# Four edits in a two-block transformer kernel: a norm's multiply on VectorE, one way to split attention weights, a reordered projection tail, and one early weight request

## The chip, the cores and the metric

The kernel runs on one core of one Trainium2 chip. The time is device microseconds of one launch, from the first to the last instruction and what lies around them; a smaller time is better.

## The reference, cut to what matters

Two model blocks run one after the other in float32. The first ends in a mixture of experts and a final norm; the second has two layers, `l = 0` and `l = 1`, each with a joint projection, attention of three kinds, an output projection and a feed-forward part.

```
# end of the first block: experts' rows are added, then the final norm
x = x + _hierarchical_moe(_rmsnorm(x, g_ffn), ...)
return _rmsnorm(x, g_final)             # x * rsqrt(mean(x*x) + eps) * g

# second block, per layer
p = h @ w_in                            # one projection for all three kinds
q_a, kv_a, dq, dk, dv, gq, gk, gv = split(p)
# mla: 4 heads; diff: 4 heads of 2 score sets; gqa: 8 query heads on 2 key heads
s = einsum('bhgqd,bhkd->bhgqk', q, k) * scale
p = softmax(s, axis=-1)
o = einsum('bhgqk,bhkd->bhgqd', p, v)
...
x = x + gate * rms(merge(o...) @ w_out)
x = x + gate * rms((silu(h @ w_gate) * (h @ w_up)) @ w_down)
```

The second block works on 768 rows in layer 0 (512 tokens and 256 context rows, six tiles of 128) and, for queries, on 512 rows (four tiles) in layer 1.

## The kernel before, in words

**Products.** A float32 product is done as three TensorE matmuls on operands split into a rounded high part and a low part (`mm3`: L99 high by high, L100, L101 the two mixed ones). A weight chunk of 128x2048 comes by a DMA on SP's queue into a buffer `raw` (L70); ScalarE copies it to `whi` (L81), VectorE subtracts to get `wlo` (L82). There are three buffers each of `raw`, `whi` and `wlo`. `ahead` asks for a chunk and splits it before its user is written; the user then finds it. Activations are split by `split`: ScalarE copies the high part (L91), VectorE subtracts (L92), both reading the same PSUM tile.

**Order.** Each engine runs its instructions in one fixed order, which a scheduler decides when the kernel is built, from the order of the code, the dependencies and the pools of buffers. So an edit in one place can move rows on several engines.

**End of the first block** (`combine`, `final`, `turned` in `moe`). For each of four token tiles, `combine(t)` adds the experts' rows (L1077) and, for two halves of 512 columns, adds a product from PSUM (L1037), sums the squares on ScalarE (L164), multiplies by the gain of the final norm on GpSimd (L1039), and sums the squares again. `final(t)` turns the sums into scales by a chain of 128x1 and 128x2 operations on VectorE (L1045 to L1051, with `rinv` L149 to L159); `turned(t)` transposes the normed tile on TensorE (`trp`, L131) into the second block's `hTx`. These run interleaved with products for the context rows.

**The projection** (`project`). Weight chunks 0 to 7 of `w_in` each give columns of `p` for six row tiles (`rows(g, tiles, ev)`; product tiles `prj`). Rows are brought into form on VectorE (`rope2`: L1431 to L1434, names `grow`, `drow`, `rp`) and written to a scratch array in DRAM, from which attention loads them (`p_d`). At the tail, a generator `gen` makes the first attention head (unit 0): it loads its rows, transposes q and k (`tp<-ident,raw`) and splits them (`mhi`, `mlo`). Chunk 3 gives the differential keys, chunk 4 the differential values (`vrow`, L1699). In this stage PSUM has six or seven tiles for products and transposes.

**Attention** (`attention`, `pipeline`). A layer has 20 units (4 mla, 8 diff, 8 gqa). For each unit, `scores` makes `sn` in PSUM, VectorE takes the maximum (L1903, L1911), ScalarE the exponentials `pn` (L1906); `turned` transposes `pn` in groups of 128x512 into a PSUM tile `tp` and splits it; `products` multiplies the two parts by the values (`pv`, L1955). There are three PSUM tiles of the kind `tp`, two `sn`, one `pv`. A unit has seven groups in layer 0 and six in layer 1. A table decides how a group is split:

```
if self.SPLITS[6 if t0 else k]:
    e = self.copies[0]
    self.copies.append(self.copies.pop(0))
    nc.scalar.activation(e, p, AF.Copy)
    nc.vector.tensor_copy(eh, e)
    nc.gpsimd.tensor_tensor(el, e, eh.bitcast(F), op=OP.subtract)
else:
    self.split(eh, el, p)
```

In the first way ScalarE copies PSUM to SBUF (L1938), VectorE casts (L1939) and GpSimd subtracts (L1940): four of seven groups in layer 0 and three of six in layer 1, 140 groups in all. The other 120 go by `split`.

**Hand-over to the next layer** (`ffn`, then `post` and the next `project`). The feed-forward part ends with a skewed loop over row tiles: down product, residual and norm (`post`), transposition into the next layer's `hT`. With layer 0, the first products of the next projection (chunks of `w_in2[1]`) follow the tiles as they come; their weights are requested on SP's queue behind the residual rows (`raw<-x_d`, `raw<-c_d`, L1383).

Of the kernel before, what the change touches and what calls it, by code (L numbers as in the profile page):

```python
# [8 lines left out]
F = mybir.dt.float32  # L9
R = mybir.dt.float32r  # L10
I32 = mybir.dt.int32
AF = mybir.ActivationFunctionType
OP = mybir.AluOpType
# [24 lines left out]
class Kern:  # L38
# [734 lines left out]
    def moe(self):  # L773
        nc, ph, sm = self.nc, self.ph, self.small
# [85 lines left out]
        el = L[:, :, 4:20].rearrange("p t (g e) -> p t g e", g=4)  # L860
# [112 lines left out]
        def places():  # L973
# [3 lines left out]
        bufs = (ph.tile([128, 1], I32, name="pix"), *places(), self.s8("praw", [2048], F),  # L977
                [self.mm("pmm0"), self.mm("pmm1")])
# [26 lines left out]
        y15, g2 = [], []  # L1005
# [19 lines left out]
        def combine(t):  # L1025
            for k in range(2):
                self.tc.keep_in_program_order(self.add_rows(xr[t], g2[t][:, k], main[k][1][:, t]))
            if t < 2:
                self.first_w[5 + t] = self.pair(raws[5 + t], k=8, pin=True)
            if t < 3:  # L1030
                self.context_products((7, 5, 6)[t], self.first_w)
            for c in range(2):
                cs = slice(c * 512, c * 512 + 512)
                x = xr[t][:, cs]
                p = self.mm("cmb")
                nc.tensor.matmul(p, spread[:self.CAP, t], y15[0][:self.CAP, cs], start=True, stop=True)
                nc.vector.tensor_tensor(x, x, p, op=OP.add)  # L1037
                self.sumsq(x, 512, fss[:, t, 0, c:c + 1])
                nc.gpsimd.tensor_tensor(x, x, y15[1][:, cs], op=OP.mult)  # L1039
                self.sumsq(x, 512, fss[:, t, 1, c:c + 1])  # L1040

        def final(t):
# [460 lines left out]
    def project(self, l, hT, new, nq, gq, qa, factors, stages=()):  # L1503


        nc = self.nc
        p_d = self.p_d
        tiles = range(6) if l == 1 else range(4)

        def rows(g, tiles, evac, w=None):  # L1510
            wh, wl = w or self.W(self.i["w_in2"][l, g], k=8, steps=4 if g > 4 else 1)
            for t in tiles:
                p = self.mm("prj")[:, :256]
                ts = slice(t * 128, t * 128 + 128)
                for kt in range(8):
                    hi, lo = (h[kt // 4][:, kt % 4, ts] if isinstance(h, list) else h[:, kt, ts] for h in hT)
                    self.mm3(p, hi, lo, wh[:, kt], wl[:, kt], kt == 0, kt == 7)
                evac(t, p)
            return wh, wl
# [93 lines left out]
        for t0 in (0, 4):  # L1613
            n = min(4, 6 - t0)
            c = slice(t0 * 128, (t0 + n) * 128)
            for k in range(3):
                if k < 2 and t0 >= nq:
                    continue
                p = self.mm("trp")
# [8 lines left out]
        for t in range(nq):  # L1628
            p = self.mm("qb")[:, :384]
# [11 lines left out]
        for t in range(6):  # L1641
            p = self.mm("kvb")
# [4 lines left out]
            pe = kv[:, t:t + 1, 128:]  # L1647
            if t < 4:
                pe = self.small.tile([128, 1, 32], F, name="kpe", bufs=2)
# [10 lines left out]
        raw = self.wp.tile([128, 2048], F, name="raw", tag="raw", bufs=self.NRAW)  # L1660
# [26 lines left out]
                out(t, col, o.rearrange("p h d -> p (h d)"))  # L1687

        differential(3, self.DK)
        while True:  # L1690
            try:
                next(gen)
            except StopIteration as e:
                self.unit0 = e.value
                break

        def ev_v(t, p):
            o = self.t5("vrow")[:, :256]
            nc.scalar.activation(o, p, AF.Copy)  # L1699
            out(t, self.DV, o)  # L1700
        rows(4, tiles, ev_v)


    def load_rows(self, pool, name, col, n, tiles=6, tag="rw"):
# [51 lines left out]
    def attention(self, l, yB, ap, nq):  # L1756

        nc = self.nc
# [7 lines left out]
        for _ in range(2):  # L1766
            hi, lo = (self.wp.tile([128, 4, 512], R, name="pe" + nm, tag="w" + nm, bufs=self.NW) for nm in ("hi", "lo"))
            self.pairs8 += [(hi[:, j], lo[:, j]) for j in range(4)]
        raw = self.wp.tile([128, 4, 512], F, name="pe", tag="raw", bufs=self.NRAW)
        self.copies = [raw[:, j] for j in range(4)]  # L1770

        self.fold = ap.tile([128, 64], F, name="fold")
        nc.vector.tensor_tensor(self.fold, self.ident[:, :64], self.ident[:, 64:], op=OP.add)
# [83 lines left out]
            nc.vector.tensor_tensor(y, y, r[:, t, :, None].to_broadcast([128, 4, 64]), op=OP.mult)  # L1857
            nc.vector.tensor_tensor(y, y, gd[:, None, :].to_broadcast([128, 4, 64]), op=OP.mult)

    SPLITS = (1, 0, 1, 0, 1, 0, 1)
    LAG = 5

    def pipeline(self, units, nq, ap):


        nc = self.nc
# [53 lines left out]
        def turned(u):  # L1922

            P, rec = probs.pop(u)
            o = ap.tile([128, 768], F, name="oT", bufs=2)
            for t0, n, k0 in groups:
                N = n * 128
                for k in range(k0, 6, 512 // N):
                    p = self.mm("tp")
                    for a in range(512 // N):  # L1930
                        for t in range(n):
                            self.tr(p[:, a * N + t * 128:a * N + t * 128 + 128], P[t0 + t][:, (k + a - k0) * 128:(k + a - k0) * 128 + 128])
                    eh, el = self.pairs8[0]
                    self.pairs8.append(self.pairs8.pop(0))
                    if self.SPLITS[6 if t0 else k]:
                        e = self.copies[0]
                        self.copies.append(self.copies.pop(0))
                        nc.scalar.activation(e, p, AF.Copy)  # L1938
                        nc.vector.tensor_copy(eh, e)  # L1939
                        nc.gpsimd.tensor_tensor(el, e, eh.bitcast(F), op=OP.subtract)  # L1940
                    else:
                        self.split(eh, el, p)
                    parts.append((u, t0, N, k, k0, eh, el, o, rec))
                    yield

# [109 lines left out]
    def ffn(self, l, hT, hp, nq):  # L2055
        nc = self.nc
# [23 lines left out]
        with self.pool("f_w") as fp:  # L2080
# [32 lines left out]
                    begun.append(g)  # L2113

            parts = [(hids[g], weight(g)) for g in (9, 10)]
            xs = self.residuals(l, "f", nq)
            gt = self.gates(l, "f", nq, hp)
            turns = []
# [135 lines left out]
```

## Time and profile before

| what | value |
|---|---|
| three runs, in order of size | 2999.06, 3010.52, 3013.27 us (median 3010.52) |
| the profiled execution | 3001.12 us, span 2999.3 us |
| TensorE busy | 2852.1 us, 95% of the span |
| VectorE, ScalarE, GpSimd busy | 1768.6, 1296.2, 413.1 us |
| mean granted clock of TensorE | 0.975 of full speed |

Times in the rows are microseconds from the start of the span. PE is TensorE's matmul, PEld its weight load, DVE VectorE, ACT ScalarE, POOL GpSimd, SP the engine whose queue issues most DMAs. A row of a timeline gives start, length, engine, line, operation, output and inputs, and in brackets how long the engine had been idle and what ended that. What ended the idle time is written as `<-DVE pelo L92`: the engine, tile and line of the instruction whose semaphore came last.

### The profile page before, as it was taken

Reading aid. Unit: us, or ns where it says so; the run is one execution under the profiler, and the core shown is the slowest. Engines: PE = TensorE matmul, PEld = TensorE weight load, DVE = VectorE, ACT = ScalarE, POOL = GpSimd, SP = SyncE. Lnnn points to the kernel's source line nnn. Section 1 sums busy time; section 2 is a strip of 40 time slices with the busy share of each in tenths; the row PEclk is TensorE's granted clock in tenths of the full one; section 3 lists DMA queues with packets and bytes.
Section 4 is the critical chain, followed back from the end, with each engine's and each line's share of the span. In section 5 each row is a group of like instructions: output and inputs, shape, how many; then the busy total and the mean of one; then the engine's idle time right before and its main releaser. Section 6 shows DMA issues by size and latency. Waiting matters only on the chain. (4 is left out here: it accounts for less than half of the span.)

```text
span 2999.3 us, 44707 instructions
## 1 busy us (share of the span) xinstructions
PE 2852.1 (95%) x17896; PEld 2463.1 (82%) x17896; DVE 1768.6 (59%) x3239; ACT 1296.2 (43%) x2275; POOL 413.1 (14%) x430
## 2 busy tenths in 40 slices
PE   8999999999799988999999999999988999899998
PEld 6997777769788878887789888888788777888887
DVE  6653344346588877789857343434565787644445
ACT  3222243234477765388745111212342787432222
POOL 2200010000110023156410000000010454000000
PEclk9999999999899999999999999999989999899999
DMA  5443464364799972421013121211233310322221
GB/s 201 141 145 138 150 207 161 142 225 168 262 388 385 351 275 87 146 78 27 4 71 141 71 71 56 71 57 71 77 127 101 106 24 3 141 99 105 92 98 71
DMA packets 130084, 399.78 MB, mean 133 GB/s; under 512 B 62199, under 2 KB 74887, under 8 KB 93128
## 3 DMA queue, kind: packets, MB, share of 16 engines
q1 hardware_dynamic: 116206, 350.04, 32.7%
q0 software_dynamic: 13520, 46.55, 4.6%
q8 instruction: 143, 2.34, 0.3%
q14 instruction: 71, 0.58, 0.1%
q10 hardware_dynamic: 144, 0.26, 0.0%
HBM read 356.64 MB, written 39.39 MB: 132 GB/s over the span
## 5 line engine op out<-in xcount | busy, mean ns | idle before, releaser
L82 DVE TENSOR_TENSOR wlo<-raw,whi 128x2048 fp32r<-128x2048 f32 (+2 forms) x203 | 421.2, 2077 | 292.9 <-ACT whi L81 292.4
L81 ACT ACTIVATE whi<-raw 128x2048 fp32r<-128x2048 f32 (+2 forms) x203 | 351.4, 1739 | 493.7 <-PE fd L101 128.6
L101 PE MATMUL fg<-hT,wlo 128*128 128x512 f32 (+1 forms) x1120 | 386.4, 345 | 0.0
L100 PE MATMUL fg<-hT,whi 128*128 128x512 f32 (+1 forms) x1120 | 386.2, 345 | 0.0
L99 PE MATMUL fg<-hT,whi 128*128 128x512 f32 (+1 forms) x1120 | 386.2, 345 | 0.0
L99 PEld LDWEIGHTS fg<-hT,whi 128*128 128x128 f32 x1120 | 211.1, 189 | 29.3
L100 PEld LDWEIGHTS fg<-hT,whi 128*128 128x128 f32 x1120 | 210.7, 188 | 29.3
L101 PEld LDWEIGHTS fg<-hT,wlo 128*128 128x128 f32 x1120 | 210.8, 188 | 29.0
L1940 POOL TENSOR_TENSOR pelo<-pe,pehi 128x512 fp32r<-128x512 f32 x140 | 181.4, 1298 | 192.0 <-DVE pehi L1939 187.5
L2106 DVE TENSOR_TENSOR sg<-sg,fg 128x512 f32<-128x512 f32 (+1 forms) x70 | 40.1, 573 | 282.1 <-PE fg L101 282.1
L101 PE MATMUL fd<-whi,hl 128*128 128x512 f32 x440 | 173.2, 394 | 0.0
L100 PE MATMUL fd<-wlo,hh 128*128 128x512 f32 x440 | 172.5, 392 | 0.0
L99 PE MATMUL fd<-whi,hh 128*128 128x512 f32 x440 | 171.2, 389 | 0.0
L1903 DVE TENSOR_REDUCE smx<-sn 128x1 f32<-128x768 f32 x160 | 151.8, 950 | 19.1 <-PE sn L1897 18.3
L2073 DVE TENSOR_TENSOR acc<-acc,fd 128x512 f32<-128x512 f32 x180 | 120.8, 686 | 65.1 <-PE fd L101 65.1
L131 PE MATMUL tp<-ident,pn 128*128 128x128 f32 x960 | 150.8, 276 | 4.1 <-DVE pelo L92 2.8
L1906 ACT ACTIVATE pn<-sn,smx 128x768 f32<-128x768 f32 x160 | 144.0, 905 | 19.7 <-DVE smx L1903 16.1
L99 PE MATMUL eg<-whi,xt 128*96 128x256 f32 x512 | 147.0, 287 | 0.0
L100 PE MATMUL eg<-wlo,xt 128*96 128x256 f32 x512 | 145.1, 283 | 1.5 <-DVE wlo L82 1.5
L101 PE MATMUL eg<-whi,xt 128*96 128x256 f32 x512 | 144.9, 283 | 0.0
L82 DVE TENSOR_TENSOR wlo<-rawx,whi 128x2048 fp32r<-128x2048 f32 x58 | 133.0, 2292 | 20.0 <-ACT whi L81 20.0
L1955 PE MATMUL pv<-pehi,vp 128*128 128x512 f32 (+1 forms) x280 | 124.3, 447 | 8.7 <-ACT oT L1959 7.8
(658 smaller groups left out, 7552.0 us busy)
## 6 DMA issues: line engine op xcount, KB each, us to landing
raw<-in_w_in SPq DMA_DIRECT2D x53, 1024.0 KB, 5.3
raw<-in_w_ada SPq DMA_DIRECT2D x48, 1024.0 KB, 5.1
raw<-in_f_gate SPq DMA_DIRECT2D x22, 1024.0 KB, 4.8
raw<-in_f_up SPq DMA_DIRECT2D x22, 1024.0 KB, 4.8
raw<-in_f_down SPq DMA_DIRECT2D x22, 1024.0 KB, 4.8
rawx<-in_e_gate SPq DMA_DIRECT2D x19, 1024.0 KB, 9.1
rawx<-in_e_up SPq DMA_DIRECT2D x19, 1024.0 KB, 9.0
rawx<-in_e_down SPq DMA_DIRECT2D x18, 1024.0 KB, 8.6
```

Source lines behind the costliest of these rows:

```text
L81: keep(nc.scalar.activation(hi[:, c], raw[:, c], AF.Copy))
L82: keep((eng or nc.vector).tensor_tensor(lo[:, c], raw[:, c], hi[:, c].bitcast(F), op=OP.subtract))
L99: t.matmul(ps, lh, rh, start=first, stop=False)
L100: t.matmul(ps, lh, rl, start=False, stop=False)
L101: t.matmul(ps, ll, rh, start=False, stop=last)
L131: self.nc.tensor.transpose(out, in_, self.ident[:k, :k])
L1903: nc.vector.tensor_reduce(m[:, t:t + 1], p[:, :768], axis=AX.X, op=OP.max, negate=True)
L1906: nc.scalar.activation(P[t], p[:, :768], AF.Exp, bias=m[:, t:t + 1], accum_out=su[:, t:t + 1])
L1940: nc.gpsimd.tensor_tensor(el, e, eh.bitcast(F), op=OP.subtract)
L1955: nc.tensor.matmul(p, v[:, k + a], e[:, a * N:a * N + N], start=k == k0 and a == 0 and e is eh, stop=k + a == 5 and e is el)
L2073: nc.vector.tensor_tensor(acc[:, t, cs], acc[:, t, cs], p, op=OP.add)
L2106: nc.vector.tensor_tensor(sg, sg, pp[1], op=OP.mult)
```

## The change

1. In `combine` the multiply by the final norm's gain goes from GpSimd to VectorE.
2. In `pipeline` the table and the three-engine way are gone: all groups go by `split`. The `raw` buffer that held the copies is not taken.
3. In `project` the values (chunk 4) are written ahead of the rest of the first head's generator, which advances one step after each of the last three row tiles, and runs to its end after them.
4. In `ffn` of layer 0, chunk 7 of the next `w_in` is asked for by `ahead` before the residual rows.

```
-                nc.gpsimd.tensor_tensor(x, x, y15[1][:, cs], op=OP.mult)
+                nc.vector.tensor_tensor(x, x, y15[1][:, cs], op=OP.mult)
...
         differential(3, self.DK)
-        while True:
-            try:
-                next(gen)
-            except StopIteration as e:
-                self.unit0 = e.value
-                break
...
-        rows(4, tiles, ev_v)
+
+        def first_head():
+            self.unit0 = yield from gen
+
+        head = first_head()
+        w = None
+        for t in tiles:
+            w = rows(4, [t], ev_v, w)
+            if t >= tiles[-1] - 2:
+                next(head, None)
+        for _ in head:
+            pass
...
-        raw = self.wp.tile([128, 4, 512], F, name="pe", tag="raw", bufs=self.NRAW)
-        self.copies = [raw[:, j] for j in range(4)]
...
-    SPLITS = (1, 0, 1, 0, 1, 0, 1)
...
-                    if self.SPLITS[6 if t0 else k]:
-                        e = self.copies[0]
-                        self.copies.append(self.copies.pop(0))
-                        nc.scalar.activation(e, p, AF.Copy)
-                        nc.vector.tensor_copy(eh, e)
-                        nc.gpsimd.tensor_tensor(el, e, eh.bitcast(F), op=OP.subtract)
-                    else:
-                        self.split(eh, el, p)
+                    self.split(eh, el, p)
...
             parts = [(hids[g], weight(g)) for g in (9, 10)]
+            if l == 0:
+                self.ahead(("w_in2", (1, 7), 8))
             xs = self.residuals(l, "f", nq)
```

What the edits do to the order of rows, at three places. First VectorE, inside one diff unit of layer 0's attention; `pelo` is a group's low part, `pehi` its high part, `pe` the copy in SBUF, `smx` a row maximum. Before:

```order
1307 L1919 RECIPROCAL srec<-ssum 128x6
1308 L1903 TENSOR_REDUCE smx<-sn 128x1
1309 L1939 CAST pehi<-pe 128x512 x2
1310 L92 TENSOR_TENSOR pelo<-tp,pehi 128x512
1311 L1903 TENSOR_REDUCE smx<-sn 128x1
1312 L1939 CAST pehi<-pe 128x512
1313 L1903 TENSOR_REDUCE smx<-sn 128x1
```

And after, at the same place of the next diff unit:

```order
1309 L1919 RECIPROCAL srec<-ssum 128x6
1310 L92 TENSOR_TENSOR pelo<-tp,pehi 128x512 x2
1311 L1903 TENSOR_REDUCE smx<-sn 128x1
1312 L92 TENSOR_TENSOR pelo<-tp,pehi 128x512
1313 L1903 TENSOR_REDUCE smx<-sn 128x1
1314 L92 TENSOR_TENSOR pelo<-tp,pehi 128x512
1315 L1903 TENSOR_REDUCE smx<-sn 128x1
```

Every cast has become a subtraction that reads the PSUM tile; the maxima stand between them as before.

Second TensorE, at layer 0's projection tail; `tp<-ident,raw` transposes the first head's rows, `prj` are the products. Before, all twelve stood together ahead of the 96 value products that close the projection:

```order
6856 L100 MATMUL prj<-wlo,hTx 128x256
6857 L101 MATMUL prj<-whi,hTx 128x256
6858 L131 MATMUL tp<-ident,raw 96x128 x12
6859 L99 MATMUL prj<-whi,hTx 128x256
6860 L100 MATMUL prj<-wlo,hTx 128x256
```

After, the first four come behind 48 products of the values (which stood from row 6859 on before), two behind the next 24, and the last six behind another 24. The first of the three places:

```order
6905 L100 MATMUL prj<-wlo,hTx 128x256
6906 L101 MATMUL prj<-whi,hTx 128x256
6907 L131 MATMUL tp<-ident,raw 96x128 x4
6908 L99 MATMUL prj<-whi,hTx 128x256
6909 L100 MATMUL prj<-wlo,hTx 128x256
```

The products of two row tiles have moved ahead of the first transposes.

Third SP's queue, at the end of layer 0's feed-forward part; `raw<-in_w_in` are the next projection's weights, `x_d` and `c_d` the residual rows. Before:

```order
360 L70 DMA raw<-in_f_down 128x2048 x2
361 L1383 DMA raw<-x_d 128x1024 x4
362 L1383 DMA raw<-c_d 128x1024 x2
363 L70 DMA raw<-in_w_in 128x2048 x6
364 L1522 DMA p_d<-gvrow 128x128 x5
```

And after:

```order
363 L70 DMA raw<-in_f_down 128x2048 x2
364 L70 DMA raw<-in_w_in 128x2048
365 L1383 DMA raw<-x_d 128x1024 x4
366 L1383 DMA raw<-c_d 128x1024 x2
367 L70 DMA raw<-in_w_in 128x2048 x6
```

One request has moved ahead of the residual rows, and six still stand behind them: chunk 7 is asked for twice, since its last two row tiles are written in a later call.

## Rows read from the trace of the kernel before

**Rows 1.** The page's first part: busy time, share, instructions by engine.

```profile
PE 2852.1 (95%) x17896; PEld 2463.1 (82%) x17896; DVE 1768.6 (59%) x3239; ACT 1296.2 (43%) x2275; POOL 413.1 (14%) x430
```

**Rows 2.** Waits of PE, whole span: total us, times, longest.

```profile
PE trp L131 <- ACT yg L1053: 6.8, 1, 6.8
...
PE prj L99 <- ACT whi L81: 5.2, 1, 5.2
...
PE pv L1955 <- POOL pelo L1940: 1.4, 1, 1.4
```

**Rows 3.** Busy time in the two attention stretches, layer 0 then layer 1.

```profile
1261.00:1531.00 270.00, 246.84 (x1684) 212.53 (x1684) 225.14 (x369) 218.37 (x497) 139.11 (x119) 0.99 0.17 45
2334.00:2553.00 219.00, 206.48 (x1326) 168.84 (x1326) 181.68 (x317) 175.21 (x357) 107.17 (x97) 0.99 0.17 48
```

**Rows 4.** The page's costliest groups: GpSimd's subtraction in attention.

```profile
L1940 POOL TENSOR_TENSOR pelo<-pe,pehi 128x512 fp32r<-128x512 f32 x140 | 181.4, 1298 | 192.0 <-DVE pehi L1939 187.5
```

**Rows 5.** VectorE's cast by line: shortest, median, longest in ns.

```profile
L1939 DVE CAST pehi<-pe x140: 382/421/1549, 1274.4 to 2547.4; 128x512 fp32r<-128x512 f32 x140
```

**Rows 6.** VectorE's groups in layer 0's attention: busy us, mean ns.

```profile
L1939 DVE CAST pehi<-pe 128x512 fp32r<-128x512 f32 x80 | 47.6, 600 | 7.0 <-ACT pe L1938 6.4
L92 DVE TENSOR_TENSOR pelo<-tp,pehi 128x512 fp32r<-128x512 f32 x60 | 40.8, 680 | 2.2 <-ACT pehi L91 2.1
```

**Rows 7.** The same in layer 1's attention.

```profile
L1939 DVE CAST pehi<-pe 128x512 fp32r<-128x512 f32 x60 | 28.1, 468 | 5.8 <-ACT pe L1938 5.2
L1800 DVE CAST dqst<-dqrow 128x256 fp32r<-128x256 f32 x8 | 8.5, 1066 | 0.0
...
L1800 DVE CAST dkst<-dkrow 128x384 fp32r<-128x384 f32 x8 | 2.8, 353 | 0.0
```

**Rows 8.** Waits of PE in layer 0's attention.

```profile
PE sn L1897 <- ACT pn L1906: 4.9, 10, 1.4
PE pv L1955 <- ACT oT L1959: 4.1, 3, 2.9
PE tp L129 <- DVE pelo L92: 3.3, 3, 1.4
PE tp L131 <- DVE pelo L92: 2.8, 4, 1.0
...
PE tp L1968 <- DVE pelo L92: 0.8, 2, 0.6
```

**Rows 9.** GpSimd's multiply at the first block's end, by line.

```profile
L1039 POOL TENSOR_TENSOR x<-x,y x8: 1260/1298/2314, 1111.7 to 1150.1; 128x512 f32<-128x512 f32 x8
```

**Rows 10.** VectorE's timeline there, and a 128x512 multiply later in the kernel.

```profile
1132.72 1.12 DVE L149 TENSOR_SCALAR fin_v<-fv 128x2 f32<-128x2 f32 x1
1133.88 0.17 DVE L150 TENSOR_SCALAR fin_y<-fin_v 128x2 int32<-128x2 int32 x1
...
2147.76 0.69 DVE L2078 TENSOR_TENSOR acc<-acc,gt 128x512 f32<-128x512 f32 x1
```

**Rows 11.** The projection tail, layer 0: busy time of one stretch, then PE.

```profile
1244.00:1248.00 4.00, 1.47 (x7) 0.88 (x8) 3.96 (x11) 0.75 (x2) 0.75 (x1) 0.88 0.50 172
...
1245.27 0.61 PE L131 MATMUL tp<-ident,raw 128*96 128x128 f32 x4 [2.04 <-DMA raw<-p_d]
```

**Rows 12.** The projection tail, layer 1: timelines of PE and DVE.

```profile
2310.57 1.06 PE L131 MATMUL tp<-ident,raw 128*96 128x128 f32 x4 [5.60 <-issue]
...
2309.65 0.42 DVE L1431 TENSOR_TENSOR drow<-prj,rope 128x256 f32<-128x256 f32 x1
```

**Rows 13.** The hand-over to layer 1: SP's queue, then ACT.

```profile
2164.02 42.66 SPq L70 DMA_DIRECT2D raw<-in_w_in  x6
...
2171.76 2.19 ACT L81 ACTIVATE whi<-raw 128x512 fp32r<-128x512 f32 x4 [3.19 <-DMA raw<-in_w_in]
2174.12 0.46 ACT L1369 ACTIVATE pre<-trp,mod,pre_a 128x128 f32<-128x128 f32 x1 [0.18 <-PE trp L131]
...
2200.49 2.18 ACT L81 ACTIVATE whi<-raw 128x512 fp32r<-128x512 f32 x4
```

## The prediction

> **What bounds the kernel now.** The page's first part comes first: TensorE is busy 95% of the span, VectorE 59% [rows 1]. Some 147 us of the 2999.3 us span are left in which TensorE does nothing, so edits that touch other engines can only pay where TensorE waits for them, or where its clock falls after a wait. The waits of TensorE tell where that is [rows 2]: one wait of 6.8 us for `yg` at the end of the first block, one of 5.2 us for the split of a weight chunk in the hand-over to layer 1, and a single one of 1.4 us for GpSimd's subtraction in attention, although that subtraction takes 181.4 us of GpSimd's time [rows 4]. GpSimd's own time there hides nearly whole. What remains is its effect on VectorE.
>
> Next the busy time in the two attention stretches [rows 3]. In 270.0 us of layer 0 TensorE is busy 246.8, VectorE 225.1, ScalarE 218.4; in 219.0 us of layer 1 it is 206.5, 181.7 and 175.2. So no engine is free: TensorE leads, the two others run at some 80%, and a unit's work passes from one to the other through three transposed tiles in PSUM. TensorE's idle time is 23.2 us in the one and 12.5 us in the other, 35.7 us together: no gain in attention can be much beyond that.
>
> **The norm's multiply.** Eight GpSimd operations of about 1.30 us (one 2.31) go [rows 9], and eight VectorE multiplies of one size with the 0.69 us of a later line come [rows 10]. VectorE gets 8 x 0.69 = 5.5 us more. Against this stand the places where VectorE was held: a 128x2 operation takes 0.17 us, and the same kind takes 1.12 us when it begins just after GpSimd's multiply [rows 10]. With some five such places of about 0.95 us that gives 4.8 us back; VectorE's sum is about even. The chain is what gets shorter: sum of squares, multiply, sum of squares runs twice per tile, and each multiply is 1.30 - 0.69 = 0.6 us shorter. Ahead of the 6.8 us wait for `yg` lie two multiplies of its own tile and two held operations: 2 x 0.6 + 2 x 0.95 = 3.1 us. The bounds are 0, if a multiply that queues on VectorE behind other work gives it all back, and 5 us if the half clock behind the wait shortens too. I take -3.
>
> **One way to split.** ScalarE does the same (a copy becomes a copy). GpSimd loses 140 subtractions. VectorE loses 140 casts and gets 140 subtractions of 0.68 us. The casts cost 600 ns in layer 0 and 468 ns in layer 1, means over 80 and 60 [rows 6, 7], while the shortest is 382 and the median 421 ns [rows 5]. So VectorE gets 80 x 0.08 + 60 x 0.21 = 6.4 + 12.8 = 19 us more. What it gets back: other casts that GpSimd holds, such as `dqst` at 1066 ns against 353 ns for the larger `dkst` in the same stretch, 8 x 0.71 = 5.7 us [rows 7]. The net is about +13 us of 407 us, on an engine with 82 us of idle time there [rows 3]: it fits.
>
> Two effects on TensorE are left. A PSUM tile was given back after ScalarE's copy, and now after VectorE's subtraction. In layer 0, the 60 groups that already go this way made TensorE wait 3.3 + 2.8 + 0.8 = 6.9 us [rows 8], 0.115 us a group; in layer 1 its waits hold none for that. For the 80 groups of layer 0 that change, this gives 80 x 0.115 = +9.2 us, for the 60 of layer 1 none. If the three tiles are now all held behind VectorE it may be twice that, +18. On the other side, VectorE is no longer held for up to 1.55 us by a neighbour (the longest cast), and its results come in steadier steps. The waits that hang on VectorE through ScalarE, `pn` and `oT`, are 4.9 + 4.1 us in layer 0 [rows 8], and the low part comes without GpSimd's 1.30 us [rows 4]; if these 9.0 us and the 1.4 us for GpSimd go, that is -10, and with the small stalls that no row names perhaps half of all idle time, -15. I take 0 between +18 and -15: the likely loss (+9) and the likely gain (-10) are of one size.
>
> The row of the longest cast shows a lock rather than a slower engine: 0.42 us alone, 1.3 to 1.55 us beside GpSimd [rows 5]. The Trainium skill, SBUF — State Buffer, section "Who interferes with whom", says that a VectorE cast in a two-port mode, or an operation with two SBUF inputs, is fully blocked while a GpSimd operation that reads SBUF holds the shared port, and that one with at most one SBUF input outside those modes is not. The trace agrees in the cast's two lengths; by that rule the subtraction from PSUM, with one SBUF input, is never held, and the first rival below would be the likelier outcome.
>
> **The values ahead of the first head.** In layer 0, TensorE is busy 1.47 of the 4 us from 1244 on, its first transposes having waited 2.04 us for a DMA, but VectorE is busy 3.96 of these 4 us [rows 11]. The products written ahead need a PSUM tile and a free row buffer each, and both come free through VectorE (`drow`). TensorE then does the products of two row tiles in place of the wait, and waits for VectorE behind them. In layer 1 the 5.60 us wait ends at 2310.57, just after VectorE's first `drow` operation of 0.42 us began at 2309.65 [rows 12]: what ended it was a PSUM tile. The value products need the same tile. So no gain there. The keys' splits now stand directly ahead of the first scores, which costs about one subtraction of 0.68 us [rows 6] in each layer. Bounds: -7.6 us (both waits, 2.0 + 5.6, hidden), +1.4 us (2 x 0.68); I take 0, the rows of VectorE being nearest.
>
> **The early weight request.** Before, the next layer's first chunk is requested at 2164.02 and split from 2171.76 on, in four steps that take ScalarE 2.19 us [rows 13], and TensorE waits 5.2 us for it [rows 2]. After, it lies ready, and products of the first two tiles fill this wait. But chunk 7 is still asked for a second time for its last two row tiles, and that split stands on ScalarE at the same place, ahead of the `pre` of 2174.12 [rows 13], which waits behind it in any case. The next transposes hang on that. What surely goes is the last of the splits ahead of the remaining products, the 2.18 us of 2200.49 [rows 13], which moves up by one request. I take -2; bounds 0 and -7.4 (5.2 + 2.2).
>
> **The sum.** -3 + 0 + 0 - 2 = -5 us. On the profiled execution of 3001.1 us this gives 2996. That execution and the three runs (2999.1, 3010.5, 3013.3) have a mean of 3006.0; less 5, 3001 us is my forecast. The three runs lie 14 us apart, 0.5%, so under 0.5% (15 us) a difference cannot be told from none; a "faster" must fall below 2995.5.
>
> **The rivals.** (A) Attention runs steadier: the lock on VectorE gone outweighs the longer hold of PSUM, -15 us in place of 0, 2986 us. For it: the 600 ns casts and their 1.55 us extreme [rows 5, 6]. Against: TensorE hardly waits on that path now [rows 2]. (B) The waits really are hidden, in the projections -7.6 and at the hand-over -7.4 in place of -2: -18 in all, 2988 us. Against: VectorE is full in one and PSUM holds the other [rows 11, 12]. (C) Slower: each transposed PSUM tile waits for VectorE's queue in attention, +18 us, and with -5 from the other parts the sum is +13, 3019 us; a median of 0.5% more, 3025.6, needs +25 in attention, 0.63 us in each of 40 units. For it: TensorE already waits 6.9 us on that path in layer 0 [rows 8]. It decides from the point at which a group costs over 0.115 us on 140 groups, 16 us. (D) Nothing comes through at all, 3006 us.
>
> **How the numbers follow.** The forecast, together with (D), has 0.48; (A) 0.24; (B) 0.13; (C) 0.15. (A) and (B) lie below 2995.5; a fifth of them may end above it, since runs spread by 0.5%, and a little of the forecast ends below it: 0.8 x 0.37 + 0.05 = 0.35 for faster. A half of (C) passes 3025.6, and the forecast's own spread adds a little: slower 0.10. The rest is within 0.5%: 0.55. The range reaches to (A) and (B) and 6 us below them, for both in part, and to (C); beyond it lie a fifth of the cases, those in which (A) and (B) come whole together or attention loses more than its bound: 2980 to 3020.
>
> **What the changed profile would show.** Right: the wait for `yg` near 4 us in place of 6.8; small VectorE operations there at 0.17 us throughout; no rows of GpSimd's subtraction, and `dqst` near 0.35 us; waits of TensorE for `pelo` in layer 0 grown from 6.9 to about 16 us, with those for `pn` and `oT` smaller, and the stretches' lengths near 270 and 219 us. The 2.0 and 5.6 us waits would be found again a few microseconds later, behind the value products. The 5.2 us wait goes, and a wait for `hT` takes its place. It would be wrong, above all, if the attention stretches change by over 10 us together, either way; or if TensorE's wait at either projection's tail is gone with none behind it.

## The result, and the profile after

The changed kernel takes 2976.5 us in the median of 12 runs (2969.5 to 2984.3), the kernel before 2998.6 us in the median of 12 (2990.1 to 3013.3). The ratio is 0.9913 with a 95% interval of 0.9895 to 0.9931: 0.9% faster, some 26 us on a kernel of 3000 us. The forecast was 3001 us, the range 2980 to 3020: too slow by 24 us, with the measured time 3.5 us below the range. Of these, 7 are in the base: the four executions from which it was taken have a mean of 3006.0, and 12 runs have a median of 2998.6. The rest is a change of -26 to -22 in place of -5. All ratios are of executions in the fast state; one execution, of 7079 us, is left out by that, with all but the split path.

The first part of the page of the changed kernel answers to [rows 1]:

```profile
PE 2847.3 (96%) x17896; PEld 2463.2 (83%) x17896; DVE 1766.0 (59%) x3244; ACT 1293.1 (43%) x2272; POOL 214.7 (7%) x282
```

GpSimd has lost 198 us. VectorE's busy time has not grown, although eight multiplies were moved to it and 140 casts became longer subtractions; the prediction had it grow by 13 us in attention alone.

Where the time went is read by stages: each from the start of its first product on TensorE to the start (or end) of a later one, in the timeline. Layer 0's attention, for example, lies between the first row of `sn` and the end of the last row of `pv`. In the kernel before:

```profile
1261.16 0.50 PE L1897 MATMUL sn<-mhi 96*128 96x512 f32 x1 [0.47 <-ACT vrow L1699]
...
1527.12 0.28 PE L1955 MATMUL pv<-pelo,vp 128*128 128x256 f32 x1
```

And in the changed kernel:

```profile
1254.96 0.50 PE L1897 MATMUL sn<-mhi 96*128 96x512 f32 x1 [1.52 <-DVE mlo L92]
...
1509.74 0.28 PE L1948 MATMUL pv<-pelo,vp 128*128 128x256 f32 x1
```

That is 266.2 us before (1527.12 + 0.28 - 1261.16) and 255.1 after. All stages that differ, taken so from the profiles, with a second profile of either kernel (runs described below) beside it:

| stage | before, twice | after, twice |
|---|---|---|
| norm: first `cmb` to first `prj` | 32.3, 32.3 | 28.4, 28.4 |
| projection of layer 0: first `prj` to first `sn` | 119.8, 121.5 | 119.9, 119.9 |
| attention of layer 0 | 266.2, 267.4 | 255.1, 255.3 |
| feed-forward of layer 0: first to last `fg` | 519.3, 518.7 | 525.7, 519.3 |
| hand-over: last `fg` to first `prj` of layer 1 | 40.4, 40.5 | 34.9, 35.0 |
| projection of layer 1: first `prj` to first `sn` | 161.7, 158.2 | 159.7, 159.3 |
| attention of layer 1 | 217.7, 217.7 | 212.5, 212.4 |

So the norm gives 3.9 us, layer 0's attention 11 to 12, layer 1's 5.3, and hand-over and projection of layer 1 together 4 to 7. The feed-forward stage of layer 0, of which no instruction was changed, took 519 or 526 us, within one kernel too; it is left out of the reasoning and comes back at the end.

In layer 0's attention these are the waits of TensorE in the changed kernel, to be laid beside [rows 8]:

```profile
PE sn L1897 <- ACT pn L1906: 5.9, 13, 1.5
PE sn L1897 <- DVE mlo L92: 1.5, 1, 1.5
PE pv L1948 <- ACT oT L1952: 1.3, 2, 0.9
PE tp L131 <- DMA mkrow<-p_d: 1.3, 1, 1.3
PE tp L131 <- DVE pelo L92: 0.9, 3, 0.5
```

The reader should see the last line. The wait for `pelo` was to grow from 6.9 us to about 16, since 140 groups give back their PSUM tile by that subtraction in place of 60. It has shrunk to 0.9. What VectorE does there, beside [rows 6]:

```profile
L92 DVE TENSOR_TENSOR pelo<-tp,pehi 128x512 fp32r<-128x512 f32 x140 | 94.3, 683 | 7.6 <-ACT pehi L91 7.0
...
L1803 DVE CAST dqst<-dqrow 128x384 fp32r<-128x384 f32 x8 | 3.2, 398 | 0.0
...
L1803 DVE CAST dkst<-dkrow 128x384 fp32r<-128x384 f32 x8 | 2.8, 350 | 0.0
```

In layer 1 the cast `dqst` went from 1066 ns [rows 7] to 487:

```profile
L1803 DVE CAST dqst<-dqrow 128x256 fp32r<-128x256 f32 x8 | 3.9, 487 | 0.0
```

The 140 subtractions all take 0.68 us, and the other casts have come down.

### The profile page after: what moved, and what is told of

The parts are those of the page before. It is cut to its first block, busy times and chain, and to the rows that moved or that the text cites. A ratio compares the mean times of both kernels' runs of the same rounds, so it can differ in the third digit from the quotient of the medians.

```text
span 2976.6 us, 44654 instructions
## 1 busy us (share of the span) xinstructions
PE 2847.3 (96%) x17896; PEld 2463.2 (83%) x17896; DVE 1766.0 (59%) x3244; ACT 1293.1 (43%) x2272; POOL 214.7 (7%) x282
## 5 line engine op out<-in xcount | busy, mean ns | idle before, releaser
L82 DVE TENSOR_TENSOR wlo<-raw,whi 128x2048 fp32r<-128x2048 f32 (+1 forms) x200 | 420.5, 2104 | 292.1 <-ACT whi L81 291.7
L81 ACT ACTIVATE whi<-raw 128x2048 fp32r<-128x2048 f32 (+1 forms) x200 | 351.0, 1762 | 495.0 <-PE fd L101 132.2
L92 DVE TENSOR_TENSOR pelo<-tp,pehi 128x512 fp32r<-128x512 f32 x260 | 175.0, 683 | 13.9 <-ACT pehi L91 11.8
L91 ACT ACTIVATE pehi<-tp 128x512 fp32r<-128x512 f32 x260 | 153.8, 601 | 44.9 <-PE tp L131 43.6
L1903 DVE TENSOR_REDUCE smx<-sn 128x1 f32<-128x768 f32 x160 | 151.7, 949 | 12.7 <-PE sn L1897 11.7
```

Source lines behind the costliest of these rows:

```text
L81: keep(nc.scalar.activation(hi[:, c], raw[:, c], AF.Copy))
L82: keep((eng or nc.vector).tensor_tensor(lo[:, c], raw[:, c], hi[:, c].bitcast(F), op=OP.subtract))
L91: nc.scalar.activation(hi, src, AF.Copy)
L92: nc.vector.tensor_tensor(lo, src, hi.bitcast(F), op=OP.subtract)
L1903: nc.vector.tensor_reduce(m[:, t:t + 1], p[:, :768], axis=AX.X, op=OP.max, negate=True)
```

## The experiments

The theory after the result (the **lock theory**): VectorE's operations whose inputs lie in SBUF were held while GpSimd worked, and the engine runs in order, so a held cast made the maxima and the subtractions behind it late; that was the cause of TensorE's waits for `pelo`. Two rivals: the **chain theory** (the low part comes sooner by two engines than by three) and the **buffer or order theory** (a free weight buffer, or another order of the rows on all engines). All ratios are to the kernel before, run on the same chip.

### One split path alone

```
-                    if self.SPLITS[6 if t0 else k]:
...
-                    else:
-                        self.split(eh, el, p)
+                    self.split(eh, el, p)
```

> The kernel before with the one split path alone (the raw buffer of the copies not taken either). If attention carries the change, as the stretches of the two traces say (11.2 us shorter in layer 0, 5.2 us in layer 1), this comes out 14 to 19 us below before. If the gain comes from the four parts together, through another order of the rows, it is under 8 us.

Measured: ratio 0.9942 (0.9922 to 0.9962), 17 us. Layer 0's attention took 254.8 us, as in the changed kernel; layer 1's 215.5, 2.2 less than before. So this part makes the gain in layer 0, and two thirds of the whole.

### All but the split path

```
+    SPLITS = (1, 0, 1, 0, 1, 0, 1)
...
+                    if self.SPLITS[6 if t0 else k]:
+                        e = self.copies[0]
```

> The changed kernel with the table and the three-engine way put back: norm, values first and early request remain. Attention theory: 3 to 7 us below before, the 3.9 us of the norm's stage and little else. Order theory: over 10 us below.

Measured: 0.9956 (0.994 to 0.9972), 13 us (8 to 18). This is more than the 3 to 7 us of the attention theory, and the number alone is that of the order theory (over 10). The stages say otherwise: the norm's stage is 28.4 us, layer 0's attention 263.5, hand-over and projection of layer 1 194.8 together (202.0 and 198.7 before), layer 1's attention 216.3. These are parts of some 4, 3 to 4, 4 to 7 and 1.4 us at the places of the three edits that remain and right behind them, which the prediction had at 5 together.

### The norm alone

```
-                nc.gpsimd.tensor_tensor(x, x, y15[1][:, cs], op=OP.mult)
+                nc.vector.tensor_tensor(x, x, y15[1][:, cs], op=OP.mult)
```

> The kernel before with the norm's multiply on VectorE alone. By the sum of the prediction 3 us below before; by the trace of the changed kernel 3.9 us in that stage. If this part carries less than 1 us, the stage's gain came from the other rows that moved there.

Measured: 0.9978 (0.9964 to 0.9993); its interval, 2 to 11 us, holds the 3.9 us by which the stage is shorter (28.4 us, in each of the eight profiles with this edit; 32.3 in each of the six without it). This is the changed kernel's VectorE at the place of [rows 10]:

```profile
1130.17 0.16 DVE L157 TENSOR_TENSOR fin_t<-fin_y 128x2 f32<-128x2 f32 x1
1130.25 0.68 DVE L1039 TENSOR_TENSOR x<-x,y 128x512 f32<-128x512 f32 x1
1130.85 0.15 DVE L158 TENSOR_TENSOR fin_t<-fin_t,fin_v 128x2 f32<-128x2 f32 x1
```

And TensorE's wait, 6.8 us before [rows 2]:

```profile
1132.92 1.94 PE L131 MATMUL trp<-ident,yg 128*128 128x128 f32 x8 [5.30 <-DVE yg L1062]
1135.04 0.58 PE L99 MATMUL prj<-whi,hTx 128*128 128x256 f32 x1 [0.19 <-ACT hTx L1374]
```

The multiply takes 0.68 us and the small operations beside it 0.16: none is held.

### The cast from PSUM, with GpSimd kept

This takes the lock from the 140 casts and leaves the three engines in their chain: VectorE makes the high part as the maximum of the PSUM tile and its copy, which is the same value, and has one input in SBUF.

```
-                        nc.vector.tensor_copy(eh, e)
+                        nc.vector.tensor_tensor(eh, p, e, op=OP.max)
                         nc.gpsimd.tensor_tensor(el, e, eh.bitcast(F), op=OP.subtract)
```

> The kernel before, with the three engines kept (ScalarE copies, VectorE makes the high part, GpSimd subtracts), but VectorE's operation is a maximum of the PSUM tile and its copy, the same value, about 0.68 us and with one SBUF input, in place of the cast from SBUF. Lock theory (VectorE's casts are held by GpSimd, and what stands behind them is late): the gain of the one split path comes nearly whole, 10 to 17 us below before, with GpSimd still as busy. Chain theory (the low part comes sooner by two engines in place of three): the chain has three engines as before, so 0 to 10 us above before.

Measured: 0.9969 (0.9952 to 0.9985), 9 us, a little under the lock theory's lower bound and on the other side of zero from the chain theory. VectorE in layer 0's attention:

```profile
L1939 DVE TENSOR_TENSOR pehi<-tp,pe 128x512 fp32r<-128x512 f32 x80 | 54.2, 683 | 5.2 <-ACT pe L1938 4.8
...
L1717 DVE CAST vp<-vr 128x384 fp32r<-128x384 f32 x6 | 6.2, 1030 | 0.0
```

And TensorE's waits there:

```profile
PE tp L131 <- DVE pehi L1939: 1.3, 3, 1.0
...
PE tp L131 <- DVE pelo L92: 0.9, 3, 0.4
```

The operation is longer than the cast (0.683 against 0.600 us in the mean), VectorE has more to do (227.2 us in the stage, 222.4 before), and the stage is 6.6 us shorter (259.6 us): what counts is not its mean length but that it is never held (0.64 to 0.69 us in all 140 cases). The 6.9 us of waits for `pelo` went down to 0.9, and another 1.3 came for `pehi`. These 1.3 us are the price, for the 80 groups, of giving the PSUM tile back by VectorE, which the prediction put at 9.2. The remaining casts from SBUF are still held, 1030 ns for `vp`. The Trainium skill, SBUF — State Buffer, section "Who interferes with whom", says that a VectorE operation in a two-port mode, or with two SBUF inputs, contends with a GpSimd operation that reads SBUF, and that one with at most one SBUF input outside those modes does not. The trace agrees with both halves: up to 1.55 us for a cast of 0.42 [rows 5], and none of the 140 `pehi` here, with one PSUM tile and one SBUF input, above 0.69.

### The split path, with GpSimd kept busy

```
                     self.split(eh, el, p)
+                    if (1, 0, 1, 0, 1, 0, 1)[6 if t0 else k]:
+                        nc.gpsimd.tensor_tensor(self.idle[0], self.idle[1], eh.bitcast(F), op=OP.subtract)
```

> The changed kernel with one added GpSimd subtraction of 128x512 for each of the 140 groups, from the group's high part into a scratch tile that nobody reads. So GpSimd is as busy as before, but it stands in no chain, and VectorE's subtraction reads PSUM. Lock theory: the 140 subtractions stay at 0.68 us, only the small casts beside them (rows of queries, keys and values) are held again; attention gets longer by 3 to 9 us, about what the run with the cast from PSUM still lacked (layer 0 near 260 us in place of 255, layer 1 near 216 in place of 212.5). Chain theory: what was lacking there was the third engine in the chain, so this run is within 2 us of the changed kernel.

Measured: 0.9924 (0.9897 to 0.995), against 0.9913 for the changed kernel; the two cannot be told apart by their times. By the stage they can: layer 0's attention is 262.1 us in place of 255.1, TensorE waits for `pelo` again, and some of VectorE's operations on SBUF are held again. TensorE's longest wait in that stretch:

```profile
PE tp L131 <- DVE pelo L92: 4.3, 7, 1.1
```

VectorE's groups of this kernel there, with the subtractions unheld and a multiply on SBUF held:

```profile
L92 DVE TENSOR_TENSOR pelo<-tp,pehi 128x512 fp32r<-128x512 f32 x140 | 94.3, 682 | 8.7 <-ACT pehi L91 8.0
...
L1863 DVE TENSOR_TENSOR yB<-yB,dif_y 128x256 f32<-128x256 f32 x6 | 4.1, 704 | 0.0
```

And GpSimd's added work, as long for each as the old subtraction:

```profile
L1940 POOL TENSOR_TENSOR pe<-pe,pehi 128x512 f32<-128x512 f32 x80 | 103.7, 1297 | 93.5 <-ACT pehi L91 92.1
```

The multiply `yB<-yB,dif_y` takes 412 ns in the changed kernel (2.4 us for six). This added work stands in no chain, so the chain theory's "within 2 us" fails in this stage. But the 7.0 us are not all GpSimd's. TensorE is idle 13.5 us of the stage, against 11.0 in the changed kernel, and busy 248.5 us, against 244.1, mostly because in two stretches its granted clock was at the lower of its two levels (0.50, 1.2 GHz). The first row is the stage, the others are the two stretches (behind the length stand the busy times of PE, PEld, VectorE, ScalarE and GpSimd, then the granted clock):

```profile
1259.76:1521.85 262.09, 248.54 (x1674) 214.60 (x1675) 223.79 (x366) 215.50 (x495) 136.38 (x118) 0.97 0.16 41
1261.50:1271.70 10.20, 8.39 (x32) 6.94 (x31) 5.11 (x9) 5.49 (x10) 0.99 (x1) 0.50 0.70 177
1292.20:1295.60 3.40, 3.40 (x14) 3.08 (x14) 3.36 (x5) 0.95 (x3) 2.66 (x2) 0.50 0.21 49
```

The run with everything on VectorE, which has no GpSimd work at the start, was at 1.2 GHz as long there (from 1255.20, below), so nothing shows that the added work lowered the clock. An estimate of what the clock costs here is 2.5 us: the first 50 instructions of TensorE in the stage took 13.7 us, against 12.6 in the changed kernel, and a stretch like the second made the 50 instructions there take 12.7 us in the kernel before, against 11.3 at full clock in the run with the norm alone. That leaves some 4.5 us for GpSimd's work. In layer 1 the stage is 213.2 us, as in the changed kernel (212.5): there the added work costs nothing, which the lock theory did not expect.

### The same at half the width, and the buffer alone

The first halves the added work (128x256 each), the second takes the buffer through attention with no work in it.

```
-                        nc.gpsimd.tensor_tensor(self.idle[0], self.idle[1], eh.bitcast(F), op=OP.subtract)
+                        nc.gpsimd.tensor_tensor(self.idle[0][:, :256], self.idle[1][:, :256], eh[:, :256].bitcast(F), op=OP.subtract)
```

> The changed kernel with 140 added GpSimd subtractions as before, but half as wide (128x256, some 0.65 us each). If what lengthens attention is the time in which GpSimd holds VectorE, about half of the 7.0 us of the full width is left in layer 0 (near 258 to 259 us in place of 262.1 and 255.1). If it is the buffer that the added work holds, or a dependency of it, the stretch stays near 262.

```
+        idle = self.wp.tile([128, 4, 512], F, name="pe", tag="raw", bufs=self.NRAW)
+        nc.gpsimd.memset(idle, 0.0)
...
         self.pipeline(units, nq, ap)
+        nc.gpsimd.memset(idle[:, 0, :1], 0.0)
```

> The changed kernel with the buffer that held the copies taken through attention, and nothing done in it but a fill at the start and one at the end. Lock theory: layer 0's attention within 2 us of 255.1. Buffer theory (what was gained came from the third weight buffer free in attention, as the last weights were asked for earlier): near 262 us.

Measured: 0.9922 (0.99 to 0.9944) and 0.9909 (0.9883 to 0.9934). Layer 0's attention is 258.5 us with half the work, 253.6 with the buffer alone. From 255.1 the half width costs 3.4 us and the full one 7.0, as was expected of a price in proportion to GpSimd's time, but the 7.0 is so near to twice 3.4 in part by luck: some 2.5 us of it are the clock's, as estimated above, and the half width, with the clock lower for no longer than in the changed kernel, has none of that:

```profile
1259.91:1518.39 258.48, 245.09 (x1674) 211.45 (x1675) 219.32 (x366) 215.23 (x495) 92.31 (x118) 0.99 0.17 42
```

So the price grows with GpSimd's work, and that it does so in proportion is not shown. The buffer costs nothing there (10.7 us idle); the buffer theory is out for layer 0.

### The values first, and the request first, each alone

```
+        for t in tiles:
+            w = rows(4, [t], ev_v, w)
+            if t >= tiles[-1] - 2:
+                next(head, None)
```

> The kernel before with the values ahead of the first head alone. By the prediction 0 (between -7.6 and +1.4). By the traces of the changed kernel and of the one with all but the split path: some 2 us off at layer 1's tail and some 2 to 3 us off at the start of layer 0's attention, so 2 to 6 us below before.

```
+            if l == 0:
+                self.ahead(("w_in2", (1, 7), 8))
```

> The kernel before with the early weight request alone. By the prediction 2 us below before: the wait of 5.2 us goes, and most of it comes back as waits for the next tiles. If the wait is really hidden, 5 to 8 us below. If it is given back whole, within 1 us of before.

Measured: 0.9981 (0.9958 to 1.0004) and 0.9989 (0.9969 to 1.001); neither can be told from no change. By stage the first has 264.7 us in layer 0's attention (266.1 to 267.4 in four profiles without it and with the old way to split), the second a hand-over of 35.0 us and a projection of layer 1 of 161.8.

### Everything on VectorE, tried as a faster version

The subtractions that GpSimd still did in attention (`dqst`, `dkst`, `gqst`, `gk`, `vp`) go to VectorE as well.

```
-                nc.gpsimd.tensor_tensor(st[:, :nt, lo], rr, st[:, :nt, 0].bitcast(F), op=OP.subtract)
+                nc.vector.tensor_tensor(st[:, :nt, lo], rr, st[:, :nt, 0].bitcast(F), op=OP.subtract)
```

> The changed kernel with the remaining GpSimd subtractions of attention (the low parts of query, key and value rows, some 74 of them) on VectorE too. Lock theory: the casts ahead of them come at 0.35 us in place of up to 1.4, which pays for half of the 25 to 30 us of work that VectorE gets; VectorE has 80 us idle there, so within 5 us of the changed kernel, more likely below than above. Chain theory: also same.

Measured: 0.9906 (0.9881 to 0.9932), the same as the changed kernel. Its two attention stretches, and the stretch of the first in which the granted clock was at 1.2 GHz:

```profile
1253.67:1511.88 258.21, 246.70 (x1674) 213.21 (x1675) 228.50 (x403) 215.16 (x495) 0.53 (x1) 0.98 0.16 41
2319.80:2536.51 216.71, 203.43 (x1326) 168.81 (x1326) 191.95 (x354) 174.74 (x356) 0.00 (x0) 1.00 0.16 44
1255.20:1265.40 10.20, 8.64 (x33) 7.11 (x31) 5.43 (x9) 5.48 (x11) 0.00 (x0) 0.50 0.70 181
```

VectorE is busy 228.5 and 192.0 us (218.3 and 183.8 in the changed kernel, below), and the stages are 258.2 and 216.7 us long, 3 to 4 us more. In layer 0 some 0.8 us of that is the clock (the first 50 instructions of TensorE took 13.4 us, against 12.6); in layer 1 the clock was full. So what is left of the lock costs no more than the work that it would take to remove it.

### Either kernel once more

> The kernel before once more, for how much a stage's length changes from one execution to the next: layer 0's attention within 1.5 us of 266.2, the norm's stage within 0.1 us of 32.3; the feed-forward stage of layer 0, where kernels with the same instructions there took 518 or 526 us, at either.

> The changed kernel once more, for the same: layer 0's attention within 1.5 us of 255.1, the norm's stage within 0.1 us of 28.4, the feed-forward stage of layer 0 at 518 or 526 us.

These are the second numbers of the table above: attention and norm repeat within 1.1 and 0.1 us, hand-over and projection of layer 1 together within 3.4, and the feed-forward stage is at 519 us in both, at 526 us in the first profile of the changed kernel.

## Why the prediction was wrong

**What bounds the kernel.** Right as far as it went: the gain in attention, some 16 us, stays under the 35.7 us of TensorE's idle time (32.1 between the stages' own bounds).

**The norm's multiply: right.** -3 was forecast, 3.9 measured; the two mechanisms named (0.6 us less per multiply, no small operation held) are both in the rows. The wait itself shrank only from 6.8 to 5.3 us, not to 4. The second wait behind it, 1.24 us before and 0.19 after, gave another 1 us, and 1.2 us came from the waits ahead of it (2.4 us for the split of a weight chunk before, one of 1.2 for `ctxsq` after), which the prediction did not count. Of its "some five" held operations the trace has four.

**One way to split: wrong, and here the forecast fell.** The failing step is "In layer 0, the 60 groups that already go this way made TensorE wait 3.3 + 2.8 + 0.8 = 6.9 us [rows 8], 0.115 us a group", with +9.2 us worked out from it for the other 80. It took these waits for the price of giving a PSUM tile back by VectorE. They were, for the most part, the price of what stood ahead of `pelo` in VectorE's queue. This is the kernel before in one unit, VectorE first, then GpSimd:

```profile
1404.00 1.30 DVE L1939 CAST pehi<-pe 128x512 fp32r<-128x512 f32 x1
1405.23 0.94 DVE L1903 TENSOR_REDUCE smx<-sn 128x1 f32<-128x768 f32 x1
1406.10 0.79 DVE L1837 CAST gqst<-gqr 128x384 fp32r<-128x384 f32 x1
1406.81 0.68 DVE L92 TENSOR_TENSOR pelo<-tp,pehi 128x512 fp32r<-128x512 f32 x1
...
1402.37 2.65 POOL L1940 TENSOR_TENSOR pelo<-pe,pehi 128x512 fp32r<-128x512 f32 x2 [2.89 <-DVE pehi L1939]
```

GpSimd worked from 1402.37 to 1405.02 on two subtractions. The cast of 0.42 us took 1.30 and ended 0.28 us after them, and the `pelo` three rows behind it ended at 1407.49; TensorE waited for it:

```profile
1407.54 0.36 PE L129 MATMUL tp<-identr,gk 128*128 128x128 f32 x2 [0.56 <-DVE pelo L92]
```

With no cast to be held, the same 60 groups cost 0.9 us (the cast from PSUM), and so do all 140 (the split path). So the term of +9.2 did not exist, and rival (A), which had 0.24, was the outcome: -16 us by the stages, -17 by the run. The gain of -10 to -15 that the prediction set against the loss came in its size, but only in part from the waits that it named: those for `oT` fell from 4.1 to 1.3 us, those for `pn` rose from 4.9 to 5.9, and most of the gain, 6.0 us, is the wait for `pelo` itself. The step "So VectorE gets 80 x 0.08 + 60 x 0.21 = 6.4 + 12.8 = 19 us more", with +13 in the net, failed with it: VectorE's busy time in the two stretches from first `sn` to last `pv` was 402.8 us before (222.4 + 180.5) and 402.2 after, as the rows show, the kernel before first (VectorE is the third busy time):

```profile
1261.16:1527.40 266.24, 245.34 (x1674) 211.31 (x1675) 222.36 (x366) 216.11 (x495) 139.11 (x119) 0.99 0.16 41
2334.09:2551.78 217.69, 206.48 (x1326) 168.84 (x1326) 180.46 (x317) 173.96 (x356) 107.17 (x97) 0.99 0.17 45
...
1254.96:1510.02 255.06, 244.09 (x1674) 211.45 (x1675) 218.32 (x366) 215.27 (x495) 31.22 (x38) 0.99 0.16 42
2316.44:2528.90 212.46, 202.91 (x1326) 169.68 (x1326) 183.84 (x317) 174.54 (x356) 27.86 (x37) 1.00 0.17 45
```

Of the operations that get shorter, the prediction counted `dqst` alone. Not counted were `vp` and `gqst`, and two lines of multiplies at the end of layer 0's attention (`yB<-yB,dif_y`: 864 ns before, 412 after).

How the 11.2 us of layer 0 divide is read from TensorE's idle time, since its busy time moves with the granted clock (two executions of the kernel before differ by 0.9 us there). Idle were 20.9 us before, 14.3 with the cast from PSUM, 10.6 with the split path alone and 11.0 in the changed kernel:

```profile
1258.05:1517.64 259.59, 245.33 (x1674) 210.89 (x1675) 227.19 (x366) 215.95 (x495) 137.15 (x119) 0.99 0.16 42
...
1261.72:1516.56 254.84, 244.29 (x1674) 211.58 (x1675) 218.42 (x366) 215.41 (x495) 31.18 (x38) 0.99 0.16 39
```

So taking the lock from the 140 casts, with the chain of three engines kept, gives 6.6 us; going to the split path gives 3.7 more; and putting GpSimd's work back beside the split path costs 2.5 (3.6 without the start of the stage, where the lower clock left 1.1 us less to wait). So the chain theory is out as the main cause in layer 0: it has some 1 us at most.

**Layer 1's attention is explained in part.** It gained 5.3 us in both profiles. By its length the split path alone gave 2.2 and the cast from PSUM 0.5. The stage takes 212.4 to 213.2 us in the changed kernel and in the two with GpSimd's added work, and 215.5 to 217.2 us in six others, of which two (the buffer held, everything on VectorE) have the whole change. The rows tell most of this apart; here are the split path alone, the buffer held with a stretch of it, and all but the split path:

```profile
2324.19:2539.67 215.48, 205.80 (x1326) 172.29 (x1326) 184.54 (x317) 175.04 (x356) 27.88 (x37) 0.98 0.16 39
...
2307.79:2523.76 215.97, 206.29 (x1326) 172.28 (x1326) 183.96 (x317) 174.62 (x356) 27.93 (x37) 0.98 0.17 44
2397.70:2404.50 6.80, 6.80 (x27) 6.04 (x28) 2.90 (x7) 3.10 (x7) 1.01 (x2) 0.50 0.03 7
...
2335.20:2551.48 216.28, 205.22 (x1326) 167.45 (x1326) 180.23 (x317) 173.75 (x356) 107.16 (x97) 1.00 0.17 45
```

In the first two TensorE is idle 9.7 us, as in the changed kernel (9.6); they are longer because some 7 us of each ran at 1.2 GHz, and none of the changed kernel's stage did: 2.8 of the 3.0 us of the one lie in its first 50 instructions of TensorE, 3.4 of the 3.5 us of the other in the 200 around the stretch shown. All but the split path is at full clock too, and 1.4 us shorter than before, of which some 3 us ran at 1.2 GHz. So of the 5.3 us, 1.4 go with the clock at the start of the stage, which was full there in every kernel with the values first (and in one without), and 1.6 are idle time that goes with the split path. The other 2.3 us are TensorE's busy time at full clock (205.2 against 202.9); they come with the split path too, and their cause stays open. With the cast from PSUM and with everything on VectorE the clock is full and TensorE idles 12.7 and 13.3 us, where VectorE is busy 192.5 and 192.0 us in place of 180.5 and 183.8: more work on VectorE does not stay hidden there.

**The values first: right in layer 0's tail, and too low by what lies beyond.** TensorE waits again behind the value products, as was said; its timeline in the changed kernel:

```profile
1245.24 0.58 PE L99 MATMUL prj<-whi,hTx 128*128 128x256 f32 x1 [5.25 <-DVE mlo L95]
...
2295.68 0.36 PE L99 MATMUL prj<-whi,hT 128*128 128x256 f32 x1 [4.82 <-DVE rp L1433]
```

The first row is of layer 0's tail, the second of layer 1's. The 2.04 and 5.60 us of [rows 11, 12] became 5.25 and 4.82 us at another place, and the projection of layer 0 is as long as before. What the prediction did not count: attention then starts with its first rows in place. In the kernels with this edit and the old way to split, layer 0's attention is 263.5 and 264.7 us, some 2 us less; the wait for `mkrow` was 3.1 us before and is 1.1 and 1.6 in these two, 1.3 in the changed kernel.

**The early request: the mechanism right, the size uncertain.** The 5.2 us wait is gone, and waits for `hT`, 5.9 us before, grew in its place, as TensorE's waits from 2140 to 2200 in the changed kernel show:

```profile
PE prj L99 <- ACT hT L1374: 10.0, 4, 3.3
PE trp L131 <- DVE raw L1352: 3.2, 1, 3.2
```

The hand-over is 5.5 us shorter. Hand-over and projection of layer 1 together took 195.8 to 202.0 us in five profiles with neither edit, 197.2 and 196.8 with the one and the other, and 192.7 to 195.9 in seven profiles with both: 4 us in the mean (198.4 against 194.4), where the prediction had 2. Of these 4, only 1.3 are idle time of TensorE (22.5 against 21.2), so most of the hidden wait came back as other waits; 2.7 are its busy time, with 20 to 24 us at 1.2 GHz in place of 24 to 34. The rival of waits that are really hidden (-15 us) did not come.

## What to carry to other kernels

A wait that names an operation is not yet the price of that operation: look at what stands ahead of it in its engine's queue, and whether one of those ran three times its shortest length. A wait must not be multiplied by a number of operations before its cause is known. GpSimd's work that is hidden by its own waits still has a price where VectorE is part of a tight loop, and the price is paid by whoever waits behind VectorE; a PSUM operand in place of one in SBUF took VectorE's operation out of it here. And a stage's length is TensorE's idle time and its busy time, of which the second moves with the granted clock: look at both before a few microseconds are given a cause.

## What the hardware showed that was not expected

The products of 256 columns in layer 0's feed-forward part run at one of two paces, at full granted clock and with nothing waited for: the mean distance from one start to the next is 0.113 us in some profiles and 0.118 in others, for the same instructions (taken over the stretch from 1700 to 2000 us). Two profiles of the changed kernel had one each, and the stage's length follows (519.3 and 525.7 us). No experiment here was aimed at the cause, and it stays open; what it means is that 6 us between two profiles of this kernel say nothing until the stages are laid side by side. The first block shows the same on a larger scale: up to the first `cmb`, where no instruction was changed, the two profiles of the changed kernel took 1106.7 and 1121.8 us. In the second the granted clock was at 1.2 GHz from 420.5 to 461.4 us; in the first it was 0.92 of full speed in the mean of that stretch.
